# RWKV-7 chunk inverses folded into the chain's stationary operands, one iteration ahead of their use

## The chip, the cores and the metric

The kernel runs on one core of a Trainium2 chip. The metric is device time in microseconds (us), from the start of the program to its end, as the median of several executions. Engines are named as the profile names them: PE is the matrix engine (PEld its weight loads), DVE the vector engine, ACT the scalar engine, POOL the GpSimd engine, SP the engine that only issues transfers. Each runs its instructions in order; they wait for one another by semaphores.

## The reference

One inference step of a one-layer encoder: a gated FFN, one combined input projection, RWKV-7 beside chunk-banded attention, an output projection, a second gated FFN and a last norm. 1024 prompt rows are computed together with 8 streams of 16 rows. The change concerns RWKV-7, a recurrence over tokens for each of 8 heads with a 64x64 state `s`:

```python
def step(s, inp):
    r_t, w_t, k_t, v_t, kk_t, a_t = inp
    sa = jnp.einsum('bhvk,bhk->bhv', s, kk_t)
    s = (s * w_t[:, :, None, :] - sa[..., None] * (kk_t * a_t)[:, :, None, :]
         + v_t[..., None] * k_t[:, :, None, :])
    y_t = jnp.einsum('bhvk,bhk->bhv', s, r_t)
    return s, y_t
```

The kernel does it in chunks of L = 32 tokens. In a chunk the vectors `sa` of the tokens depend on one another through a triangular system, whose inverse (32x32 for each chunk and head) is computed beforehand.

## The kernel before, in words

Everything is written out for one core, as a program whose instructions a scheduler of the framework puts in order for each engine before the kernel runs; the order on an engine is then fixed. The stages are: first FFN, projection and preparation of RWKV, the RWKV chain beside the attention, output projection, second FFN.

**Preparation.** `_project` computes the columns of RWKV and of attention. For each pair of heads p (4) and each group of 8 chunks g (5), `_prepare_products` writes to DRAM what the chain will read: `ard` (rows that multiply the state), `grd` (the masked products of a chunk with itself: of its 64 rows 32 belong to the values, 32 to the solved vectors), `wsd` (the turned keys, also 32 rows for the values and 32 for the solved vectors) and `ad` (the triangular matrices). `_invert` loads up to 112 triangular matrices, one to a partition, inverts them on DVE in 31 steps of two instructions, and stores them as `inv`. Two of the inversions (of p = 3, and of the late groups of p = 2) come after the projection, right ahead of the chain.

**Chain.** `_rwkv` runs 10 iterations of 4 steps, so 40 steps, numbered here 0 to 39 (a step is one chunk of all 8 heads, or 4 of the 16-row streams at the end). `_rwkv_load` brings the operands of one iteration one iteration ahead: `mov` (state in rows 0 to 63, values in rows 64 to 95, solved vectors in rows 96 to 127), `wout` and `wst` (stationary operands with the same rows), and `tt`, the inverses. A step in `_rwkv_run` is: 8 products `pw` (L961) from state and values; a copy to `wx` (L963); 8 products `pu` with the inverses (L966); four copies of `pu` into rows 96 to 127 of `mov`, by DVE and ACT in turn (L969); 8 products `px` (L971) and 8 products `py` (L975); two DVE products that scale `px` into the next state (L984); a copy of `py` to `y` (L986). `pw`, `pu`, `px` lie in one bank called `ps_c`; `py` and all small helpers share one bank, `_post_bank`. `_rwkv_post` normalises the outputs of iteration i - 1 in pieces between the steps of iteration i (POOL subtracts the mean, L1024, and scales, L1032; after the last step PE turns `y`, L1038, DVE multiplies to `yo`, L1042, POOL adds, L1044, SP stores `yo`).

**What stands beside the chain.** Three iterations are written ahead of `_attention_inputs`, whose value projection (`ps_av`, L567 to L569, 432 products) fills PE between the chain's dependent steps. Then memory is freed, and `_attention` runs 74 units on it; six units are written after each further iteration. The loads of attention are issued by POOL (`_attention_load`: `q` L1081, `kt` L1087, `v` L1089, `bias` L1091); they go into memory that `ps_av` reads until its end. Transfers of the projection are issued by SP (`k.dq`) and ACT (`k.aq`); the chain's by SP.

Of the kernel before, what the change touches and what calls it, by code (L numbers as in the profile page):

```python
# [9 lines left out]
F32 = mybir.dt.float32  # L10
# [461 lines left out]
def _project(k, a):  # L472
# [50 lines left out]
    for p in range(NPAIR):  # L523
        srcs = [shifted(4 * j + p) for j in range(3)]
        _prepare_more(k)
        _rwkv_prepare(k, p, wa, *srcs)
        for q in QK[NQK * p // NPAIR:NQK * (p + 1) // NPAIR]:
            _attention_in(k, w, *q)
        if p == 1:
            _invert(k, (0, 0, NG))  # L530
        elif p == 2:
            _invert(k, (1, 0, NG), (2, 0, 2))
    _prepare_more(k)
# [260 lines left out]
def _prepare_products(k, q):  # L794
# [60 lines left out]
def _invert(k, *parts):  # L855


    nc = k.nc
    am = k.iv.tile([P, L, L], F32, tag="inv_a", bufs=k.niv, name="inv_a")
    w = k.iv.tile([P, L, L], F32, tag="inv_w", bufs=k.niv, name="inv_w")  # L860
    n, rows = 0, []
    for p, g0, g1 in parts:
        rows.append(slice(n, n + 16 * (g1 - g0)))
        n += 16 * (g1 - g0)
        nc.sync.dma_start(am[rows[-1]], k.ad[p][g0:g1].rearrange("g h c s t -> (g h c) s t"))
    nc.gpsimd.memset(w, 0.0)
    nc.gpsimd.memset(_flat(w)[:, 0:L * L:L + 1], 1.0)
    for s in range(L - 1):
        r, m = s + 1, L - 1 - s
        u = k.iv.tile([P, r, m], F32, tag="inv_t", bufs=2, name="inv_t")  # L870
        nc.vector.tensor_tensor(u[:n], w[:n, 0:r, s:s + 1].to_broadcast([n, r, m]),
                                am[:n, s:s + 1, s + 1:].to_broadcast([n, r, m]), ALU.mult)
        nc.vector.tensor_tensor(w[:n, 0:r, s + 1:], w[:n, 0:r, s + 1:], u[:n], ALU.add)
    for (p, g0, g1), r in zip(parts, rows):
        nc.sync.dma_start(k.inv[p][:, g0:g1].rearrange("s g x t -> (g x) s t"), w[r])


def _chunk_constants(k, a):
# [7 lines left out]
    for w in k.wst:  # L886
        nc.vector.tensor_copy(w[0:HD].rearrange("r p e i (h d) -> r (p e i h) d", d=HD),
                              k.ident[0:HD, None, 0:HD].to_broadcast([HD, 4 * NH, HD]))


def _rwkv_load(k, i):


# [17 lines left out]
    nc.sync.dma_start(q.wout[0:HD], k.ard[g].rearrange("(h d) c l -> d h c l", d=HD)[:, :, cj])  # L911
    nc.sync.dma_start(q.wout[HD:P].rearrange("r h c l -> r h (c l)"), k.grd[g][:, :, cj].rearrange("h r c l -> r h (c l)"))
    q.wst = k.wst[i % 2]
    for e in range(2):
        nc.sync.dma_start(q.wst[HD:P, :, e].rearrange("r p i x -> r p (i x)"),
                          k.wsd[g][:, HEADS[e], 2 * j:2 * j + 2].rearrange("p r i x -> r p (i x)"))

# [11 lines left out]
def _sample_states(k, a, j, mov):  # L929

    nc = k.nc
    for p in range(NPAIR):
        sin = k.rw.tile([P, 4, HD], F32, tag="sin", bufs=4, name="sin")
# [4 lines left out]
        nc.scalar.copy(mov[0:HD, :, 2 * p:2 * p + 2].rearrange("r b h d -> r b (h d)"),  # L938
                       ps[0:HD].rearrange("p (b x) -> p b x", x=P))


def _rwkv_run(k, a, i, pq, q, nq):
# [4 lines left out]
    q.y = rw.tile([P, 4, 2, HD], F32, tag="y", bufs=2, name="y")  # L947
    post = iter(()) if pq is None else _rwkv_post(k, i - 1, pq)
    fin = None
    if i == 7:  # L950
        fin = rw.tile([HD, 1, NH, HD], F32, tag="y", bufs=2, name="fin")
    for c in range(4):
        cc = 4 * i + c
        mov, wout = q.mov[:, c], q.wout[:, :, c]
        wst = q.wst[:, :, c % 2, c // 2].rearrange("r p (h d) -> r p h d", d=HD)
        pw, pu = (k.cbank[:, 128 * j:128 * j + 128].rearrange("p (a d) -> p a d", a=2)
                  for j in (cc % 2, 1 - cc % 2))
# [12 lines left out]
        for hh in range(NH):  # L970
# [29 lines left out]
def _state_out(k, st, dst):  # L1000
# [13 lines left out]
def _rwkv_post(k, i, q):  # L1014
# [257 lines left out]
def tile_encoder_step(ctx: ExitStack, tc: tile.TileContext, *aps):  # L1272
# [35 lines left out]
    with ExitStack() as s_rw, ExitStack() as s_xg:  # L1308
# [97 lines left out]
        with ExitStack() as s:  # L1406
# [119 lines left out]
```

## Time and profile before

| what | value |
|---|---|
| median of 3 runs | 2608.65 us (2604.74 to 2610.08) |
| time of the profiled execution | 2605.25 us |
| span of the profiled execution | 2603.5 us |
| PE busy in the span | 2422.6 us, 93% |
| DVE, ACT, POOL busy | 1124.8, 899.8, 1076.5 us |
| transfers | 284.75 MB in 230283 packets |

The span is the part of the execution between the first and the last instruction of the core; 1.75 us lie around it. Starts of instructions are counted in us from the start of the span. The granted clock (PEclk) is the mean of two levels of PE's clock, 1.00 for 2.4 GHz and 0.50 for 1.2 GHz. A busy PE isn't a PE at its peak: matmuls overlap, so what a group of matmuls holds of PE is read from its start to the start of the next group.

### The profile page before, as it was taken

The page shows a single profiled execution, that of the slowest core. Times are in us where ns is not written, and L with a number is a line of the kernel's source. Part 1 is how long each engine was busy: PE and PEld are TensorE (multiplying, and loading weights), DVE is VectorE, ACT ScalarE, POOL GpSimd, SP SyncE. Part 2 cuts the span into 40 slices and gives each one's busy share as a digit, 9 for nine tenths or more (in the row PEclk, how much of TensorE's full clock was granted, in tenths as well). Part 3 has the DMA queues.
Part 4 walks back from the last instruction along what each step waited for, and adds up shares of the span by engine and source line. Part 5 has one row for each costly group of instructions (what it writes and reads, how often), then busy time and mean ns, then how long its engine had stood idle before and what let it go on. Part 6 is the DMA issues. An engine that isn't in the chain of part 4 may idle for free.

```text
span 2603.5 us, 43481 instructions
## 1 busy us (share of the span) xinstructions
PE 2422.6 (93%) x17415; PEld 2161.5 (83%) x17415; DVE 1124.8 (43%) x2346; ACT 899.8 (35%) x1903; POOL 1076.5 (41%) x966
## 2 busy tenths in 40 slices
PE   4999999988999999999997999897999999989998
PEld 3899999986888799899874666676999999988886
DVE  6322222214544533856854666346222222225555
ACT  5333333321111443443323576524333333321112
POOL 4545454444433233443213443105554544544332
PEclk8999999999999999999996899998999999999999
DMA  3222112227322324543658994522221122252221
GB/s 113 67 68 86 56 63 86 67 83 269 113 77 70 107 63 133 168 132 104 190 148 197 219 206 112 175 91 65 67 86 57 62 86 68 69 197 102 77 102 73
DMA packets 230283, 284.75 MB, mean 109 GB/s; under 512 B 54920, under 2 KB 183552, under 8 KB 227264
## 3 DMA queue, kind: packets, MB, share of 16 engines
q1 hardware_dynamic: 194044, 226.72, 27.8%
q0 software_dynamic: 7648, 25.43, 4.1%
q10 hardware_dynamic: 28388, 29.81, 3.5%
q8 instruction: 137, 2.24, 0.4%
q14 instruction: 66, 0.54, 0.1%
HBM read 191.79 MB, written 90.12 MB: 108 GB/s over the span
## 4 chain that ended last, share of the span: by engine, by line
PE 42%; DVE 5%; POOL 3%; issue 3%; ACT 2%; DMA 2%; ACTq 0%; POOLq 0%; DVEq 0%
PE pa L341 3%; PE pd L450 3%; PE pd L451 3%; PE pd L449 3%; PE pa L343 3%; PE pa L342 3%; PE pb L341 2%; PE pb L342 2%; PE pb L343 2%; POOL frm L292 2%; PE ps_s L1132 1%; PE ps_o L1186 1%; PE ps_pt L1171 1%; PE ps_yc L975 1%; PE ps_wo L1261 1%
## 5 line engine op out<-in xcount | busy, mean ns | idle before, releaser
L341 PE MATMUL pa<-F,frm 128*128 128x256 f32 (+1 forms) x1408 | 424.6, 302 | 34.7 <-ACT r L348 25.2
L343 PE MATMUL pa<-F,frm 128*128 128x256 f32 (+1 forms) x1408 | 419.3, 298 | 2.7 <-POOL frm L292 2.7
L342 PE MATMUL pa<-F,frm 128*128 128x256 f32 (+1 forms) x1408 | 419.3, 298 | 2.1 <-POOL F L272 2.1
L453 DVE TENSOR_TENSOR x<-pd,x 128x512 f32<-128x512 f32 x396 | 270.0, 690 | 243.1 <-PE pd L451 228.8
L163 POOL TENSOR_TENSOR spl<-raw,spl 128x1024 fp32r<-128x1024 f32 x78 | 187.6, 2408 | 453.0 <-ACT spl L162 453.0
L449 PE MATMUL pd<-spl,h 128*128 128x512 f32 x792 | 314.0, 397 | 14.8 <-ACT spl L162 12.1
L450 PE MATMUL pd<-spl,h 128*128 128x512 f32 x792 | 311.9, 394 | 13.3 <-POOL spl L163 13.3
L292 POOL TENSOR_TENSOR frm<-cmb,frm 128x512 fp32r<-128x512 f32 x176 | 230.1, 1309 | 221.7 <-ACT frm L291 221.3
L343 PE MATMUL pb<-F,frm 128*128 128x320 f32 (+1 forms) x1056 | 312.7, 296 | 3.1 <-POOL frm L292 3.1
L342 PE MATMUL pb<-F,frm 128*128 128x320 f32 (+1 forms) x1056 | 312.2, 296 | 3.1 <-DVE F L271 3.1
L341 PE MATMUL pb<-F,frm 128*128 128x320 f32 (+1 forms) x1056 | 313.3, 297 | 1.2 <-ACT frm L291 1.2
L451 PE MATMUL pd<-spl,h 128*128 128x512 f32 x792 | 311.8, 394 | 0.0
L341 PEld LDWEIGHTS pa<-F,frm 128*128 128x128 f32 x1408 | 268.9, 191 | 44.4 <-ACT r L348 33.0
L343 PEld LDWEIGHTS pa<-F,frm 128*128 128x128 f32 x1408 | 269.1, 191 | 3.5 <-POOL frm L292 3.5
L342 PEld LDWEIGHTS pa<-F,frm 128*128 128x128 f32 x1408 | 269.4, 191 | 2.5 <-POOL F L272 2.5
L292 POOL TENSOR_TENSOR frm<-raw,frm 128x512 fp32r<-128x512 f32 x132 | 173.8, 1318 | 186.7 <-ACT frm L291 186.7
L162 ACT ACTIVATE spl<-raw 128x1024 fp32r<-128x1024 f32 x78 | 82.2, 1055 | 406.3 <-PE pd L451 342.7
L343 PEld LDWEIGHTS pb<-F,frm 128*128 128x128 f32 x1056 | 200.2, 190 | 3.8 <-POOL frm L292 3.8
L342 PEld LDWEIGHTS pb<-F,frm 128*128 128x128 f32 x1056 | 200.1, 190 | 3.3 <-DVE F L271 3.3
L341 PEld LDWEIGHTS pb<-F,frm 128*128 128x128 f32 x1056 | 200.0, 189 | 1.8 <-ACT frm L291 1.8
L449 PEld LDWEIGHTS pd<-spl,h 128*128 128x128 f32 x792 | 150.1, 190 | 48.5 <-ACT spl L162 12.3
L450 PEld LDWEIGHTS pd<-spl,h 128*128 128x128 f32 x792 | 150.1, 189 | 48.3 <-POOL spl L163 16.2
(259 smaller groups left out, 4572.7 us busy)
## 6 DMA issues: line engine op xcount, KB each, us to landing
raw<-in_w_ff_gate_dram SPq DMA_DIRECT2D x22, 1024.0 KB
raw<-in_w_ff_up_dram SPq DMA_DIRECT2D x22, 1024.0 KB
raw<-in_w_ff_down_dram SPq DMA_DIRECT2D x44, 512.0 KB
raw<-in_w_in_dram SPq DMA_DIRECT2D x26, 512.0 KB
hr<-hd SPq DMA_DIRECT2D x11, 1152.0 KB
hr<-he SPq DMA_DIRECT2D x11, 1152.0 KB
q<-qk POOLq DMA_DIRECT2D x24, 384.0 KB, 7.6
x<-xd SPq DMA_DIRECT2D x18, 512.0 KB
```

What stands on the lines that cost most here:

```text
L162: k.nc.scalar.activation(dst[:, 0], raw, AF.Copy)
L163: k.nc.gpsimd.tensor_tensor(dst[:, 1], raw, dst[:, 0].bitcast(F32), ALU.subtract)
L292: nc.gpsimd.tensor_tensor(d[:, 1], x, d[:, 0].bitcast(F32), ALU.subtract)
L341: nc.tensor.matmul(ps, frm[:, 0, c], F[:, 0, jj, c], start=new and c == 0, stop=False, **kw)
L342: nc.tensor.matmul(ps, frm[:, 0, c], F[:, 1, jj, c], start=False, stop=False, **kw)
L343: nc.tensor.matmul(ps, frm[:, 1, c], F[:, 0, jj, c], start=False, stop=c == 3, **kw)
L449: mm(ps, h[:, 0, f, a], d[f][:, 0, b], start=f == 0, stop=False)
L450: mm(ps, h[:, 0, f, a], d[f][:, 1, b], start=False, stop=False)
L451: mm(ps, h[:, 1, f, a], d[f][:, 0, b], start=False, stop=f == 1)
L453: nc.vector.tensor_tensor(xs, ps, xs, ALU.add)
L975: mm(py[s, hh % 2], wout[:, hh, L:], mov[:, hh], start=True, stop=True)
L1132: mm(ps, q.qs[i // 3][:, j, h, t:t + P], q.ks[h][:, c0:c0 + n], start=j == 0, stop=j == 1)
```

## The change

Products with the inverse are no longer made inside a step. Since a solved vector is the inverse times a column of `pw`, and is used only through `wst` and the right half of `wout`, the inverse can be multiplied into those operands instead: `_fold` does it for iteration i + 1 during steps 0 and 1 of iteration i, in two halves of 32 products each (`kg`, keys, 64 columns; `gq`, 32 columns), a copy of each half (`fk` by ACT, `fq` by DVE) and four transfers of each on SP that move the rows to partitions 96 to 127. `_fold_load` brings `tt`, `kg` and `gq`. A step then is `pw`, four copies on DVE alone, `px`, `py`, state. The preparation writes `gqd` (2 transfers on SP for each p and g) and `kgd` (2 on ACT), and `wsd` goes from SP to ACT; `_rwkv_load` brings half as many rows of `grd` and `wsd`. The inversion works on the transposed result, with the same element counts. Of the last inversion only loads and memsets come ahead of the chain; its DVE work is written after the chain's first iteration, and one more iteration is written ahead of the attention's inputs (4 instead of 3). Eight units are written after each iteration instead of six. Some small tiles share a buffer: `gn_sq` now lies in the buffer of `yo`, `so` in that of `sin`.

```diff
@@ _prepare_products
     for h in range(2):
+        k.dq.dma_start(k.gqd[g][L * p:L * p + L, h], gram[HD * h + L:HD * h + 2 * L, :, L:])
...
-    k.dq.dma_start(k.wsd[g][p], tb)
+    nc.scalar.dma_start(k.wsd[g][p], tb)
+    for e in range(2):
+        nc.scalar.dma_start(k.kgd[g][e, L * p:L * p + L], tb[HD * e + L:HD * e + 2 * L])
@@ _rwkv_load
-    nc.sync.dma_start(q.wout[HD:P].rearrange("r h c l -> r h (c l)"), k.grd[g][:, :, cj].rearrange("h r c l -> r h (c l)"))
+    nc.sync.dma_start(q.wout[HD:HD + L].rearrange("r h c l -> r h (c l)"), k.grd[g][:, :L, cj].rearrange("h r c l -> r h (c l)"))
@@ new
+def _fold(k, i, q):
+    nc = k.nc
+    g, j = divmod(i, 2)
+    tt, kg, gq = k.tt[g], k.kg.pop(i), k.gq.pop(i)
+    ps = _post_bank(k, "ps_f").rearrange("p (e i h d) -> p e i h d", e=2, i=2, h=2)
+    for c in range(4):
+        for h in range(2):
+            for b in range(NPAIR):
+                s = slice(L * b, L * b + L)
+                nc.tensor.matmul(ps[s, c % 2, c // 2, h], tt[s, h, 4 * j + c], kg[s, c % 2, c // 2, HEADS[h]], start=True, stop=True)
+    fk = k.rw.tile([P, 4 * P], F32, tag="fk", bufs=1, name="fk")
+    nc.scalar.copy(fk, ps.rearrange("p e i h d -> p (e i h d)"))
+    for b in range(NPAIR):
+        nc.sync.dma_start(q.wst[HD + L:P, b].rearrange("r e i x -> r (e i x)"), fk[L * b:L * b + L])
+    yield
...
@@ _rwkv_run
-        wx = rw.tile([P, 2, HD], F32, tag="wx", bufs=2, name="wx")
-        nc.vector.tensor_copy(wx, pw)
-        for hh in HEAD_ORDER:
-            s = slice(L * (hh // 2), L * (hh // 2) + L)
-            mm(pu[s, hh % 2], q.tt[s, hh % 2, c], wx[s, hh % 2], start=True, stop=True)
-        for j in range(4):
-            copy = nc.scalar.copy if j % 2 else nc.vector.tensor_copy
-            copy(mov[HD + L:P, 2 * j:2 * j + 2], pu[L * j:L * j + L])
+        for b in range(NPAIR):
+            nc.vector.tensor_copy(mov[HD + L:P, 2 * b:2 * b + 2], pw[L * b:L * b + L])
...
+        if c < 2 and nq is not None:
+            next(fold, None)
+        if c == 2 and i + 2 < 2 * NG:
+            _fold_load(k, i + 2)
@@ _rwkv_post
-    sq = rw.tile([P, NH, HD], F32, tag="gn_sq", bufs=1, name="gn_sq")
+    sq = rw.tile([P, NH, HD], F32, tag="yo", bufs=1, name="gn_sq")
@@ tile_encoder_step
+        next(chain)
+        next(chain)
+        for _ in late:
+            pass
         for _ in range(3):
             next(chain)
...
-                for _ in range(6):
+                for _ in range(8):
                     next(units, None)
```

The first place is PE inside the value projection. Of before, this is what stands from the `pu` of step 3 to two of the pieces of its `py`:

```order
L966 MATMUL ps_c<-wx,tt 32x64 x8
L567 MATMUL ps_av<-spl,xg 128x256
L568 MATMUL ps_av<-spl,xg 128x256
L569 MATMUL ps_av<-spl,xg 128x256
L567 MATMUL ps_av<-spl,xg 128x256
L975 MATMUL ps_yc<-mov,wout 32x64
L568 MATMUL ps_av<-spl,xg 128x256
L569 MATMUL ps_av<-spl,xg 128x256
L975 MATMUL ps_yc<-mov,wout 32x64
```

In the changed program there is no `pu`; here are both fold halves (`ps_f`) for iteration 1, beside step 2 of iteration 0 (L1010 is `pw`, L1014 `px`, L1018 `py`, L569 to L571 the value projection):

```order
L972 MATMUL ps_f<-kg,tt 32x64 x32
L1010 MATMUL ps_c<-mov,wout 32x64 x8
L569 MATMUL ps_av<-spl,xg 128x256
L570 MATMUL ps_av<-spl,xg 128x256
L571 MATMUL ps_av<-spl,xg 128x256
L1018 MATMUL ps_yc<-mov,wout 32x64 x8
L569 MATMUL ps_av<-spl,xg 128x256
L570 MATMUL ps_av<-spl,xg 128x256
L571 MATMUL ps_av<-spl,xg 128x256
L569 MATMUL ps_av<-spl,xg 128x256
L983 MATMUL ps_f<-gq,tt 32x32 x32
L1014 MATMUL ps_c<-mov,wst_12326 64x64 x8
```

Eight products of each step have gone, 64 of each iteration have come, and they stand in runs of 32.

The second place is POOL where the attention begins, after the projection's last work. Before:

```order
L1032 TENSOR_TENSOR y<-y,gn_s 128x512
L1081 DMA q<-qk_8741 64x4x384 x2
L1087 DMA kt<-qk_8844 64x384 x2
L1044 TENSOR_TENSOR yo<-yo,gb 128x512
L1024 TENSOR_TENSOR y<-y,gn_m 128x512
L1087 DMA kt<-qk_8844 64x384 x2
L1089 DMA v<-vd 128x3x128
L1031 TENSOR_TENSOR gn_s<-gn_s,mhalf 128x8
L1091 DMA bias<-bias_6312 128x1024
```

In the changed program the same loads (L1133 `q`, L1139 `kt`, L1141 `v`, L1143 `bias`) read so:

```order
L1091 TENSOR_TENSOR yo<-yo,gb 128x512
L1071 TENSOR_TENSOR y<-y,gn_m 128x512
L1133 DMA q<-qk_8763 64x4x384 x2
L1139 DMA kt<-qk_8866 64x384 x4
L1141 DMA v<-vd 128x3x128
L1143 DMA bias<-bias_6322 128x1024
L1133 DMA q<-qk_8763 64x4x384
L1078 TENSOR_TENSOR gn_s<-gn_s,mhalf 128x8
```

The `yo` that stood between the first loads and the others (that of iteration 1, which needs the end of iteration 2) now stands behind them.

The third place is PE where the value projection has ended. Before, the order from step 9 on is:

```order
L961 MATMUL ps_c<-mov,wout 32x64 x8
L966 MATMUL ps_c<-wx,tt 32x64 x8
L975 MATMUL ps_yc<-mov,wout 32x64 x3
L971 MATMUL ps_c<-mov,wst_12331 64x64 x8
L975 MATMUL ps_yc<-mov,wout 32x64 x5
L961 MATMUL ps_c<-mov,wout 32x64 x8
L966 MATMUL ps_c<-wx,tt 32x64 x8
L975 MATMUL ps_yc<-mov,wout 32x64 x3
```

In the changed program it is, after the `pw` and `px` of step 9 (L1184 are scores, `ps_s`, of the first units, L1223 turns the first unit's weights):

```order
L1184 MATMUL ps_s<-kt,q 128x128 x2
L972 MATMUL ps_f<-kg,tt 32x64 x32
L1010 MATMUL ps_c<-mov,wout 32x64 x8
L1184 MATMUL ps_s<-kt,q 128x128 x2
L1018 MATMUL ps_yc<-mov,wout 32x64 x8
L983 MATMUL ps_f<-gq,tt 32x32 x32
L1014 MATMUL ps_c<-mov,wst_12326 64x64 x8
L1018 MATMUL ps_yc<-mov,wout 32x64 x8
L1184 MATMUL ps_s<-kt,q 128x256 x2
L1010 MATMUL ps_c<-mov,wout 32x64 x8
L1223 MATMUL ps_pt<-ident,e 128x128
```

The scores of the third unit (128x256) stand behind 14 steps' work before (0 to 13), and behind 11 steps' work now (0 to 10).

## Rows read from the trace of the kernel before

**Rows 1.** Windows: stretch, length, busy of PE, PEld, DVE, ACT, POOL, clock, DMA share, GB/s.

```profile
1040.00:1280.00 240.00, 225.49 (x1681) 210.83 (x1680) 165.74 (x429) 98.37 (x225) 100.87 (x136) 0.99 0.47 146
1280.00:1368.00 88.00, 84.67 (x1031) 71.29 (x1035) 56.38 (x158) 16.97 (x51) 11.06 (x8) 0.98 0.63 156
1368.00:1406.00 38.00, 20.42 (x329) 14.17 (x330) 12.89 (x36) 5.32 (x19) 14.63 (x21) 0.57 0.86 192
1406.00:1617.00 211.00, 201.33 (x2638) 139.25 (x2639) 133.39 (x373) 138.35 (x365) 87.09 (x108) 0.87 0.82 185
1617.00:1661.00 44.00, 38.03 (x375) 28.03 (x371) 24.27 (x73) 36.74 (x99) 8.87 (x11) 0.96 0.40 115
```

**Rows 2.** Timeline of step 9: start, length, engine, line, what, [idle before <- releaser].

```profile
1367.92 0.43 PE L961 MATMUL ps_c<-mov,wout 96*32 96x64 f32 x16
...
1368.42 0.29 DVE L963 COPY wx<-ps_c 128x128 f32<-128x128 f32 x1 [0.55 <-PE ps_c L961]
...
1368.77 0.43 PE L966 MATMUL ps_c<-wx,tt 32*32 32x64 f32 x16 [0.41 <-DVE wx L963]
...
1369.26 0.28 DVE L969 COPY mov<-ps_c 32x128 f32<-32x128 f32 x1 [0.55 <-PE ps_c L966]
...
1369.69 0.26 ACT L969 COPY mov<-ps_c 32x128 f32<-32x128 f32 x1 [1.36 <-DVE mov L969]
...
1369.98 0.29 DVE L969 COPY mov<-ps_c 32x128 f32<-32x128 f32 x1 [0.43 <-ACT mov L969]
...
1370.31 0.26 ACT L969 COPY mov<-ps_c 32x128 f32<-32x128 f32 x1 [0.36 <-DVE mov L969]
...
1370.62 0.69 PE L971 MATMUL ps_c<-mov,wst 128*64 128x64 f32 x16
...
1371.23 0.41 PE L975 MATMUL ps_yc<-mov,wout 128*32 128x64 f32 x10
...
1372.33 0.43 PE L961 MATMUL ps_c<-mov,wout 96*32 96x64 f32 x16 [0.69 <-DVE mov L984]
```

**Rows 3.** Timeline of POOL, same columns, from the end of the value projection.

```profile
1368.01 1.49 POOL L1081 DMA_DIRECT2D q<-qk  x2
1369.49 1.07 POOL L1087 DMA_DIRECT2D kt<-qk  x2
1387.86 1.26 POOL L1044 TENSOR_TENSOR yo<-yo,gb 128x512 f32<-128x512 f32 x1 [17.30 <-DVE yo L1042]
...
1391.31 0.79 POOL L1089 DMA_DIRECT2D v<-vd  x1
...
1393.82 0.59 POOL L1091 DMA_DIRECT2D bias<-bias  x1
```

**Rows 4.** Timeline of DVE and PE where the first units begin.

```profile
1404.45 0.50 DVE L1142 TENSOR_TENSOR ps_s<-ps_s,bias 128x128 f32<-128x128 f32 x2 [3.94 <-DMA bias<-bias]
...
1405.81 0.80 PE L1132 MATMUL ps_s<-kt,q 128*128 128x256 f32 x2 [3.21 <-ACT e L1157]
```

**Rows 5.** Timeline of ACT's queue and PE in step 10.

```profile
1377.66 0.32 ACTq L583 DMA_DIRECT2D out_dram<-vt  x1
1378.03 0.26 ACT L969 COPY mov<-ps_c 32x128 f32<-32x128 f32 x1 [3.64 <-DMA out_dram<-vt]
...
1378.34 1.12 PE L971 MATMUL ps_c<-mov,wst 128*64 128x64 f32 x16 [3.15 <-ACT mov L969]
```

**Rows 6.** Timeline of PE inside the value projection.

```profile
1348.75 0.30 PE L975 MATMUL ps_yc<-mov,wout 128*32 128x64 f32 x2
...
1348.98 0.39 PE L568 MATMUL ps_av<-spl,xg 128*128 128x256 f32 x1
...
1361.48 0.43 PE L966 MATMUL ps_c<-wx,tt 32*32 32x64 f32 x16
...
1361.84 0.38 PE L569 MATMUL ps_av<-spl,xg 128*128 128x256 f32 x1
```

**Rows 7.** Timeline of PE: matmuls of 16 columns.

```profile
1480.25 0.99 PE L1194 MATMUL ps_o<-ptr,cv 128*64 128x16 f32 x26
```

**Rows 8.** Transfers from 1280 to 1660: queue, packets, MB, share of 16 engines.

```profile
q1 hardware_dynamic: 51477, 35.09, 40.0%
```

More of the change, by code (lines that the diff above doesn't have):

```diff
@@ L529, in _project @@
         if p == 1:
-            _invert(k, (0, 0, NG))
+            for _ in _invert(k, (0, 0, NG)):
+                pass
         elif p == 2:
-            _invert(k, (1, 0, NG), (2, 0, 2))
+            for _ in _invert(k, (1, 0, NG), (2, 0, 2)):
+                pass
     _prepare_more(k)
@@ L867, in _invert @@
     nc.gpsimd.memset(_flat(w)[:, 0:L * L:L + 1], 1.0)
+    yield
     for s in range(L - 1):
         r, m = s + 1, L - 1 - s
[L870 to L873, printed above, removed]
+        u = k.iv.tile([P, m, r], F32, tag="inv_t", bufs=2, name="inv_t")
+        nc.vector.tensor_tensor(u[:n], w[:n, s:s + 1, 0:r].to_broadcast([n, m, r]),
+                                am[:n, s, s + 1:, None].to_broadcast([n, m, r]), ALU.mult)
+        nc.vector.tensor_tensor(w[:n, s + 1:, 0:r], w[:n, s + 1:, 0:r], u[:n], ALU.add)
     for (p, g0, g1), r in zip(parts, rows):
@@ L911, in _rwkv_load @@
     nc.sync.dma_start(q.wout[0:HD], k.ard[g].rearrange("(h d) c l -> d h c l", d=HD)[:, :, cj])
-    nc.sync.dma_start(q.wout[HD:P].rearrange("r h c l -> r h (c l)"), k.grd[g][:, :, cj].rearrange("h r c l -> r h (c l)"))
+    nc.sync.dma_start(q.wout[HD:HD + L].rearrange("r h c l -> r h (c l)"), k.grd[g][:, :L, cj].rearrange("h r c l -> r h (c l)"))
     q.wst = k.wst[i % 2]
     for e in range(2):
-        nc.sync.dma_start(q.wst[HD:P, :, e].rearrange("r p i x -> r p (i x)"),
-                          k.wsd[g][:, HEADS[e], 2 * j:2 * j + 2].rearrange("p r i x -> r p (i x)"))
+        nc.sync.dma_start(q.wst[HD:HD + L, :, e].rearrange("r p i x -> r p (i x)"),
+                          k.wsd[g][:, HD * e:HD * e + L, 2 * j:2 * j + 2].rearrange("p r i x -> r p (i x)"))
     n = 4 * (L if g < 4 else NQ)
@@ L939, in _sample_states, with _fold_load @@
                        ps[0:HD].rearrange("p (b x) -> p b x", x=P))
+def _fold_load(k, i):
+    nc = k.nc
+    g, j = divmod(i, 2)
+    if j == 0:
+        k.tt[g] = k.rw.tile([P, 2, 8, L], F32, tag="tt", bufs=2, name="tt")
+        nc.sync.dma_start(k.tt[g].rearrange("s a c t -> s (a c t)"), k.inv[:, :, g].rearrange("b s x t -> (b s) (x t)"))
+    k.kg[i] = k.rw.tile([P, 2, 2, P], F32, tag="kg", bufs=1, name="kg")
+    nc.sync.dma_start(k.kg[i].rearrange("s e i x -> s e (i x)"),
+                      k.kgd[g][:, :, 2 * j:2 * j + 2].rearrange("e s i x -> s e (i x)"))
+    k.gq[i] = k.rw.tile([P, 2, 4, L], F32, tag="gq", bufs=1, name="gq")
+    nc.sync.dma_start(k.gq[i].rearrange("s h c l -> s h (c l)"), k.gqd[g][:, :, 4 * j:4 * j + 4].rearrange("s h c l -> s h (c l)"))
+def _fold(k, i, q):
+    nc = k.nc
+    g, j = divmod(i, 2)
+    tt, kg, gq = k.tt[g], k.kg.pop(i), k.gq.pop(i)
[9 more added lines that the diff above has]
+        nc.sync.dma_start(q.wst[HD + L:P, b].rearrange("r e i x -> r (e i x)"), fk[L * b:L * b + L])
+    yield
+    ps = _post_bank(k, "ps_f")[:, :8 * L].rearrange("p (h c l) -> p h c l", h=2, c=4)
+    for c in range(4):
+        for h in range(2):
+            for b in range(NPAIR):
+                s = slice(L * b, L * b + L)
+                nc.tensor.matmul(ps[s, h, c], tt[s, h, 4 * j + c], gq[s, h, c], start=True, stop=True)
+    fq = k.rw.tile([P, 2, 4, L], F32, tag="fq", bufs=1, name="fq")
+    nc.vector.tensor_copy(fq.rearrange("p h c l -> p (h c l)"), ps.rearrange("p h c l -> p (h c l)"))
+    for b in range(NPAIR):
+        nc.sync.dma_start(q.wout[HD + L:P, 2 * b:2 * b + 2, :, L:].rearrange("r h c l -> r (h c) l"),
+                          fq[L * b:L * b + L].rearrange("r h c l -> r (h c) l"))
 def _rwkv_run(k, a, i, pq, q, nq):
@@ L948, in _rwkv_run @@
     post = iter(()) if pq is None else _rwkv_post(k, i - 1, pq)
+    fold = _fold(k, i + 1, nq) if nq is not None else None
     fin = None
@@ L955, in _rwkv_run @@
         wst = q.wst[:, :, c % 2, c // 2].rearrange("r p (h d) -> r p h d", d=HD)
-        pw, pu = (k.cbank[:, 128 * j:128 * j + 128].rearrange("p (a d) -> p a d", a=2)
-                  for j in (cc % 2, 1 - cc % 2))
+        pw = k.cbank[:, 128 * (cc % 2):128 * (cc % 2) + 128].rearrange("p (a d) -> p a d", a=2)
         px = k.cbank[:, 256:].rearrange("p (a d) -> p a d", a=NPAIR)
@@ L961, in _rwkv_run @@
             mm(pw[s, hh % 2], wout[0:HD + L, hh, 0:L], mov[0:HD + L, hh], start=True, stop=True)
-        wx = rw.tile([P, 2, HD], F32, tag="wx", bufs=2, name="wx")
-        nc.vector.tensor_copy(wx, pw)
-        for hh in HEAD_ORDER:
-            s = slice(L * (hh // 2), L * (hh // 2) + L)
-            mm(pu[s, hh % 2], q.tt[s, hh % 2, c], wx[s, hh % 2], start=True, stop=True)
-        for j in range(4):
-            copy = nc.scalar.copy if j % 2 else nc.vector.tensor_copy
-            copy(mov[HD + L:P, 2 * j:2 * j + 2], pu[L * j:L * j + L])
+        for b in range(NPAIR):
+            nc.vector.tensor_copy(mov[HD + L:P, 2 * b:2 * b + 2], pw[L * b:L * b + L])
         for hh in range(NH):
@@ L1054, in _rwkv @@
     n = 2 * NG
+    _fold_load(k, 0)
     pq, q = None, _rwkv_load(k, 0)
     k.nc.vector.memset(q.mov[0:HD, 0], 0.0)
+    for _ in _fold(k, 0, q):
+        pass
+    _fold_load(k, 1)
+    yield
     for i in range(n):
@@ L1298, in tile_encoder_step @@
     k.wsd = [tc.dram_tile([NPAIR, P, 4, P], F32, name=f"wsd{g}") for g in range(NG)]
+    k.kgd = [tc.dram_tile([2, P, 4, P], F32, name=f"kgd{g}") for g in range(NG)]
+    k.gqd = [tc.dram_tile([P, 2, 8, L], F32, name=f"gqd{g}") for g in range(NG)]
     k.vmd = [tc.dram_tile([P, 2, NH * HD], F32, name=f"vmd{g}") for g in range(NG)]
@@ L1390, in tile_encoder_step @@
         s_pr.close()
-        _invert(k, (3, 0, 2))
-        _invert(k, (2, 2, NG), (3, 2, NG))
+        for _ in _invert(k, (3, 0, 2)):
+            pass
+        late = _invert(k, (2, 2, NG), (3, 2, NG))
+        next(late)
         k.rw = pool(s_rw, "rw")
@@ L1395, in tile_encoder_step @@
         chain = _rwkv(k, a)
+        next(chain)
+        next(chain)
+        for _ in late:
+            pass
         for _ in range(3):
```

9 lines of the change are left out of this document (3 added, 6 removed).

## The prediction

> **What bounds the kernel now.** I read the busy time by stage first. In the value projection (1280 to 1368) PE is busy 84.67 of 88 us at a clock of 0.98, though the chain runs through it: the chain's latency is covered there, and only what its instructions hold of PE counts. From 1368 to 1406 PE is busy 20.42 of 38 us, at a clock of 0.57: the cover has ended, attention hasn't begun. From 1406 to 1617 chain and attention share PE (201.33 of 211 us, clock 0.87, the transfers' engines busy 0.82), from 1617 to 1661 units stand alone [rows 1]. So a shorter chain step is worth little for itself, except in the gap of 38 us.
>
> Then I asked for the timeline of the gap. Step 9 starts at 1367.92 and step 10 at 1372.33, 4.41 us: products, copy, products, four copies that take turns on DVE and ACT, products, state [rows 2]. The gap isn't five such steps only. POOL issues `q` and two of four `kt` at 1368.01 and 1369.49, then waits 17.30 us for the `yo` of iteration 1, which has to wait for iteration 2's end, and so `v` goes out at 1391.31 and `bias` at 1393.82 [rows 3]. `bias` lands when DVE can add it, 1404.45, 10.63 us after its issue, and at 1405.81 PE takes the third unit's scores [rows 3, 4]. I call that the restart. Steps 9 to 13 are done by then (five steps), 26 remain. The chain is late too for the last cache stores that ACT issues: step 10's copy sat behind them 3.64 us [rows 5].
>
> **The change part by part.**
>
> *Removed products.* A `pu` holds PE 0.36 us (1361.48 to 1361.84) [rows 6]; 40 of them, 14.4 us.
>
> *Added folds.* A half is 32 products, 64 records, four times the 16 of a `pu` of the same shape: 4 x 0.36 = 1.44 us. For the 32 columns of the second half no row exists. Its price lies between half of that (0.72 us) and the same; 26 records of 16 columns took 0.99 us, 38 ns each, no less than the 27 ns of a record of 64 columns (0.43 us for 16) [rows 6, 7], so I take 1.44. Twenty halves hold 28.8 us: PE gets 14.4 us more work in all. Where it counts depends on the stretch.
>
> *Value projection.* The old order had 9 steps (0 to 8) in it, the new one 8 and six halves. Less 9 x 0.36 = 3.2 us and one step without `pu` (0.36 + 0.61 + 0.41 = 1.4 us: `pw` as `pu`, `px` from 1370.62 to 1371.23, ten records of `py` [rows 2]); more 6 x 1.44 = 8.6 us. Pieces of `py` that stand alone hold 0.23 us for two records (1348.75 to 1348.98 [rows 6]); the order has 54 runs of chain work between `ps_av` before and 39 now. Fifteen fewer at some 0.2 us: -3. Sum +1 us.
>
> *The gap.* In the new order POOL's loads stand ahead of that `yo`; they need the memory of `ps_av`, so they still begin at its end, which I call T0. `q` 1.49 and two `kt` 1.07 us bring the issue to T0 + 2.6 [rows 3]. With the 10.63 us of `bias` as landing time the first scores start near T0 + 12.7; four `kt`, `v` and `bias` are out by T0 + 5.0, so `bias` is there by T0 + 16. PE goes in order, so behind those first scores come two halves, step 10 and the scores between them. Steps 8 and 9 are over by then: without copy and `pu`, a step is 0.50 (to the first copy) + 3 x 0.30 + 0.31 (last copy to `px`) + 1.71 (`px` to next `pw`) = 3.4 us [rows 2]. At the lower clock `px` took 1.12 instead of 0.69 us, 1.6 times as long [rows 2, 5]. So two halves 4.6, `px` 1.1, `pw` and `py` 1.2, scores 1.3: 8.2 us, and the restart at T0 + 21. Before it came 37.9 us after the end of the cover. -17 us. From both sides: if loads land at once, the chain sets it at three steps and two halves, 13 us, -25; if `bias` and the chain's own loads (both use the same engines) land twice as late, T0 + 33, -5.
>
> *After the restart.* Before, 26 steps of 0.36 + 0.36 + 0.61 + 0.41 = 1.74 us: 45.2. Now three steps fewer have been done: 29 of 1.38 = 40.0, and twelve halves 17.3: 57.3. +12 us, if PE is the bound all through; PE idles 9.7 of 211 us there [rows 1], so the least is about +6 (halves that fill idle time, second halves at half price), the most +18 (all of it at the lower clock, 1.6 times 12 being 19).
>
> *Dependence of the chain.* Two hops fewer in each step: at most the 9.7 us of idle time are to be had. I take -2. At the restart PE runs on from the first scores nearly without pause, so the lower clock should end earlier than before; -1.
>
> *Transfers.* Gone for each iteration are 512 packets of 1 KB (half of `grd` and `wsd`); `kg` and `gq` add 512, `fk` 128 of 2 KB, `fq` 1024 of 128 bytes: +1152. The chain's queue used 40% of 16 engines over 380 us for 51477 packets, 47 ns each [rows 8]: 3.4 us of all engines for each iteration, some 20 us beyond the restart, where they are busy 0.82 of 211 us [rows 1]. There is room for it. I cost it at 0, with 0 to +12 as bounds: the cover is that prefetched loads have their time, and it is gone if folded rows land after `px` wants them.
>
> The Trainium skill, "DMA: Bandwidth & Descriptors", puts line rate at 512 bytes or more (Specifications), which speaks against the 128-byte pieces, but says in "Why small descriptors are slow (HBM only)" that transfers within SBUF are spared, a 1 MB one with 128-byte packets reaching 78% of the link. By that and its 435 GB/s, the 384 KB of `fk` and `fq` would take an estimated 1.2 us, and the sum would be the same, for the price above is already 0.
>
> *Preparation.* ACT gets three issues for each of 20 units at about 0.32 us [rows 5], 19 us, over 240 us in which it is busy 98 us and PE 225 [rows 1]; SP gets two and gives one. ACT's evacuations cover it; 0, at most +5. The late inversion has PE covered by `ps_av` as before: 0. `gn_sq` in the buffer of `yo` makes ACT wait for the store of `yo`, with exponentials queued behind it; in the order some 25 DVE instructions lie between that `yo` and the `gn_sq`, so 0; without them up to a landing time, 10 us in each of seven iterations.
>
> **Sum:** +1 - 17 + 12 - 2 - 1 = -7 us on 2605.25, the profiled execution's time: 2598. The median of the runs is 3.4 us above that execution; I keep 2598.
>
> **The rivals.**
>
> *A. The gap shrinks, and nothing is gained.* The loads of attention meet those of the chain when transfers are already at 0.86 of the engines' time [rows 1]; if landing takes as long again, the gap gives 5 to 10 us and the folds take it back: +1 - 8 + 12 - 3 = +2, about 2605 (2600 to 2610). For it: 10.63 us for one 512 KB load. Against: half of the gap before was POOL's own wait.
>
> *B. Slower, by the clock.* PE's clock was at its lower level for 2 x (1 - 0.87) = 26% of the stretch 1406 to 1617 [rows 1], after moments in which PE waited. Runs of 32 products with 32 rows and columns, in one bank that others need, add such moments: each fold waits for the bank's last copy, and `py` for the fold's. If the mean clock falls to 0.79, another 0.16 x 211 = 34 us run at the lower level and lose some 0.4 of it, 13 us: -7 + 13 = +6, 2611; at 0.75, 2618. It decides from about 0.83 down, where the gain is used up. For it: the folds' work is of that kind, and the clock already moves. Against: PE has less to wait for in each step.
>
> The Trainium skill, "TensorE: Matmul & The Clock Gate", section "A second HAM failure mode: psum-queue depth-cycling", says that PE that idles shortly between groups for its banks has its clock swing between the two levels; by that rule B is what comes. The clock of 0.87 at 95% busy agrees with it in kind.
>
> *C. More gain.* Chain and loads land early, folds fill idle time, and the clock returns sooner: -25 + 6 - 4 = -23, 2582.
>
> **How the numbers follow.** The forecast (its own range 2590 to 2603) gets 0.48, A 0.25, B 0.18, C 0.09. About 0.2%, 5.2 us, is what a measurement of this kernel can tell from no change. Faster than 2603.4: 0.42 of the forecast, a little of A, and C, 0.52. Within: 0.27; slower: 0.21. The range leaves out the ends of B and C: 2581 to 2615.
>
> **What would show it.** Right: `ps_f` halves of about 1.4 us at the full clock, 0.43 us `pu` gone; step to step 3.4 us in the gap; `bias` issued within 6 us of the last `ps_av`; the third unit's scores some 21 us after it; PE's work beyond the restart up by about 12 us. Wrong: `ps_s` waiting for `kt` or PE for folded rows far beyond that; a clock under 0.83 from the restart to the chain's end; ACT's `gn_sq` waiting for the store of `yo`; PE idle in the projection well above 14.5 of 240 us.

## The result, and the profile after

The changed kernel takes 2641.43 us (median of 4 runs, 2638.28 to 2653.09) beside 2606.69 us for the kernel before (4 runs): a ratio of 1.0143, 95% interval 1.0106 to 1.018, so about 37 us slower. The forecast was 2598 us and its range ended at 2615. The profiled execution took 2644.2 us, its span 2642.2.

The windows of the changed kernel, with the columns of [rows 1], show where:

```profile
1040.00:1280.00 240.00, 225.00 (x1706) 212.71 (x1706) 163.84 (x428) 97.62 (x225) 98.82 (x136) 0.99 0.55 157
1280.00:1368.00 88.00, 80.96 (x1176) 70.93 (x1173) 54.72 (x154) 12.74 (x32) 6.13 (x4) 0.90 0.61 147
1368.00:1406.00 38.00, 18.54 (x345) 14.55 (x341) 12.62 (x40) 3.92 (x13) 14.56 (x20) 0.60 0.78 174
1406.00:1617.00 211.00, 179.65 (x2499) 130.06 (x2498) 122.25 (x353) 110.00 (x280) 77.65 (x99) 0.79 0.80 183
```

The projection is as before. From 1406 to 1617 PE is busy 179.65 us where it was 201.33, at a clock of 0.79 where it was 0.87 [rows 1]: PE waits, while DMA is no busier (0.80 against 0.82). The last outputs of attention come at 1700.61 instead of 1659.07. PE alone shows this in the gap (timeline, columns of [rows 2]):

```profile
1371.07 0.43 PE L1010 MATMUL ps_c<-mov,wout 96*32 96x64 f32 x16
1383.68 1.22 PE L1014 MATMUL ps_c<-mov,wst 128*64 128x64 f32 x16 [12.17 <-issue]
...
1394.35 1.93 PE L972 MATMUL ps_f<-kg,tt 32*32 32x64 f32 x64 [3.15 <-DMA kg<-kgd]
...
1403.16 0.80 PE L1184 MATMUL ps_s<-kt,q 128*128 128x256 f32 x2
```

The `px` of step 8 stands 12.17 us behind its `pw`; the trace names no releaser for it. It is the first `px` of iteration 2, so it reads the rows that the fold wrote. What SP did at that time (timeline of SP's queue):

```profile
1368.20 0.78 SPq L920 DMA_DIRECT2D wst<-wsd  x2
1374.57 0.55 SPq L926 DMA_DIRECT2D gb<-gb  x1
1375.21 5.26 SPq L976 DMA_DIRECT2D wst<-fk  x4
1380.52 5.98 SPq L987 DMA_DIRECT2D wout<-fq  x4
1386.60 0.55 SPq L955 DMA_DIRECT2D kg<-kgd  x1
```

ACT had copied `fk` at 1354.16, some 20 us earlier, and its four transfers still went out from 1375.21 to 1380.47, when `px` already wanted them. The waits of SP's queue from 1360 to 1392 (total us, times, longest us) name what held it here: the landings of the last cache stores of the value projection, which ACT issues.

```profile
SPq L920 <- DMA out_dram<-vt: 14.8, 1, 14.8
SPq L926 <- DMA out_dram<-vt: 5.5, 1, 5.5
SPq L976 <- DMA out_dram<-vt: 2.8, 2, 1.5
SPq L987 <- DMA out_dram<-vt: 2.3, 1, 2.3
```

In front of `fk` (L976) stands `gb` (L926) too, but the `yo` that it waits for was done at 1372.14, 2.4 us before `gb` went out. In later iterations it is that `yo` that holds the queue (the same view from 1300 to 1700):

```profile
SPq L926 <- POOL yo L1091: 96.7, 7, 20.7
```

`gb` of iteration i + 1 goes into the buffer that `yo` of iteration i - 1 reads (two buffers), and that `yo` is the last work of iteration i. So every fold of iteration i + 1 is sent only when iteration i has ended. The chain of waits around 1450 shows the whole loop (start, length, what):

```profile
1445.08 0.42 PE ps_y L1085 x3
...
1445.76 0.90 DVE yo L1089 x4
...
1446.73 1.27 POOL yo L1091
...
1448.02 0.55 SPq L926
...
1448.61 0.67 SPq L976
...
1451.02 11.37 DMA wout<-fq
...
1462.43 0.42 PE ps_yc L1018 x2
```

From the last transposes of one iteration to the first `py` that may run in the next lie 17.35 us (1445.08 to 1462.43). Before, `gb` (L921 there) waited for the same `yo`, but only loads with an iteration of time stood behind it:

```profile
SPq L921 <- POOL yo L1044: 46.9, 7, 29.2
```

### The profile page after: what moved, and what is told of

It is laid out like the page before. It is cut to its first block, busy times and chain, and to the rows that moved or that the text cites. A ratio compares the mean times of both kernels' runs of the same rounds, so it can differ in the third digit from the quotient of the medians.

```text
span 2642.2 us, 44951 instructions
## 1 busy us (share of the span) xinstructions
PE 2428.2 (92%) x18055; PEld 2177.3 (82%) x18055; DVE 1133.3 (43%) x2396; ACT 881.7 (33%) x1833; POOL 1074.1 (41%) x966
## 4 chain that ended last, share of the span: by engine, by line
PE 68%; DMA 8%; POOL 6%; DVE 6%; issue 6%; ACT 3%; SPq 1%; ACTq 0%; POOLq 0%; DVEq 0%
PE pa L341 6%; PE pd L449 6%; PE pa L343 6%; PE pa L342 6%; PE pd L451 6%; PE pd L450 6%; PE pb L341 3%; PE pb L342 3%; PE pb L343 3%; POOL frm L292 3%; PE ps_p L226 2%; PE ps_p L228 2%; PE ps_p L227 2%; DVE cmb L297 1%; PE ps_wo L1314 1%
```

## The experiments

All ratios are to the kernel before on the same chip; 0.1% is 2.6 us. copy_chain3, copy_u6 and copy_sq stand on `fold_copy`; copy_sq_gb on copy_sq; copy_late0, copy_moves0 and copy_twice on copy_sq_gb; copy_spread on copy_moves0.

| kernel | median us | ratio, 95% interval |
|---|---|---|
| gb_late | 2627.26 | 1.0073 (1.0044 to 1.0102) |
| sq_own | 2643.71 | 1.0133 (1.0102 to 1.0163) |
| gb_sq | 2626.66 | 1.0075 (1.0052 to 1.0097) |
| fold_actq | 2620.39 | 1.0049 (1.0028 to 1.007) |
| gb_actq | 2614.26 | 1.0026 (1.0003 to 1.0049) |
| gb_sq_actq | 2609.64 | 1.0008 (0.9993 to 1.0023) |
| fold_copy | 2611.59 | 1.0024 (0.9999 to 1.0048) |
| copy_chain3 | 2612.51 | 1.0033 (1.0015 to 1.005) |
| copy_u6 | 2611.33 | 1.0014 (0.9988 to 1.0039) |
| copy_sq | 2605.7 | 0.9985 (0.9972 to 0.9999) |
| copy_sq_gb | 2601.47 | 0.9972 (0.9953 to 0.999) |
| copy_late0 | 2602.71 | 0.998 (0.9967 to 0.9994) |
| copy_moves0 | 2596.27 | 0.9959 (0.9945 to 0.9973) |
| copy_spread | 2605.14 | 0.999 (0.9974 to 1.0006) |
| copy_twice | 2667.4 | 1.0234 (1.0216 to 1.0253) |
| after_moves0 | 2641.68 | 1.013 (1.0101 to 1.0158) |
| before_sq | 2618.95 | 1.0024 (1.0005 to 1.0044) |
| before_late | 2618.74 | 1.003 (1.0016 to 1.0044) |

**gb_late, sq_own, gb_sq: which wait.** Theory Q says SP's queue, theory G the shared buffer of `gn_sq`, theory P the folds' products.

```diff
 # gb_late: out of _rwkv_load, into _rwkv_run behind the fold of the same step
+        if c == 1:
+            _gb_load(k, i, q)
 # sq_own (gb_sq has both)
-    sq = rw.tile([P, NH, HD], F32, tag="yo", bufs=1, name="gn_sq")
+    sq = rw.tile([P, NH, HD], F32, tag="gn_sq", bufs=1, name="gn_sq")
-    fk = k.rw.tile([P, 4 * P], F32, tag="fk", bufs=1, name="fk")
+    fk = k.rw.tile([P, 4 * P], F32, tag="kg", bufs=1, name="fk")
```

gb_late: 

> The changed kernel with one transfer moved: gb of an iteration is loaded in its own iteration, behind the transfers of its fold, and not one iteration ahead in front of them. Theory Q (SP's queue): the load of gb waits for the yo of two iterations before (96.7 us in 7 waits, after), and fk and fq stand behind it, so folded rows go out when px already wants them. Then px of step 8 waits under 4 us (12.17 before the edit), the chain and units end 25 to 35 us earlier, and the time is 2607 to 2617, about that of the kernel before. Theory G (gn_sq in yo's buffer): the chain of waits goes through the store of yo (four of 8 to 10 us); little changes, 2632 to 2641. Theory P (the products of the folds and the clock): within 5 us of 2641.

sq_own: 

> The changed kernel with gn_sq in a buffer of its own again; to make room fk lies in the buffer of kg, so the next kg waits for the landing of fk. Theory Q: gn_sq is late only because SP is late; 2636 to 2644. Theory G: ACT no longer waits for the store of yo, four pieces of 8 to 10 us leave the chain of waits, 2605 to 2620. Theory P: within 5 us of 2641.

gb_sq: 

> Both edits together: gb behind the folds, and gn_sq in its own buffer with fk in that of kg. Theory Q: as with gb moved alone, within 4 us. Theory G: as with gn_sq apart, or if both count, a further 8 to 20 us below the better of the two. Theory P: still 2636 or more. If neither wait remains and the terms of the forecast hold otherwise, 2595 to 2605.

Moving one load takes back about half of the loss (1.0143 to 1.0073: 18 us, 6 to 30 by the two intervals). Q holds, but not in size: 10 us above its range, and the `px` of step 8, which was to wait under 4 us, still waits 8.60 and 2.10 in gb_late (timeline of PE):

```profile
1379.65 1.67 PE L1018 MATMUL ps_c<-mov,wst 128*64 128x64 f32 x12 [8.60 <-issue]
1383.41 0.48 PE L1018 MATMUL ps_c<-mov,wst 128*64 128x64 f32 x4 [2.10 <-DMA wst<-fk]
```

So the wait of step 8 is hardly `gb`'s, and the gain comes later in the chain; that is argued from these rows, not tried apart. A buffer for `gn_sq` takes back nothing, alone or with it, so G isn't borne out here; `fk` in the buffer of `kg` may cost something of its own, which wasn't tried apart. With `gb` out of the way SP waits for the `fk` copy itself (68.0 us in 7 in gb_sq), and all its other transfers queue behind that.

**fold_actq, gb_actq, gb_sq_actq: another queue.**

```diff
-        nc.sync.dma_start(q.wst[HD + L:P, b].rearrange("r e i x -> r (e i x)"), fk[L * b:L * b + L])
+        nc.scalar.dma_start(q.wst[HD + L:P, b].rearrange("r e i x -> r (e i x)"), fk[L * b:L * b + L])
 # and so for the four of fq
```

fold_actq: 

> The changed kernel with the eight transfers of fk and fq of each iteration issued by ACT and not by SP; gb stays where it is. Theory Q: they no longer stand behind gb, but ACT issues 8 transfers per iteration at 0.33 us, 2.6 us, in front of its exponentials, and waits for DVE's fq; 2612 to 2628, so most of what moving gb gives. Theory G: 2641 or more, since ACT still waits for the store of yo. Theory P: within 5 us of 2641.

gb_actq: 

> The changed kernel with both edits of the first runs: gb behind the folds, and fk and fq issued by ACT. Theory L: gb is already out of the way when ACT issues, so nothing is gained over ACT's queue alone; what is left is the landing; 2616 to 2624. If gb in front of the other loads of SP's queue still costs: 2608 to 2615. Theory P: 2618 or more, too.

gb_sq_actq: 

> The changed kernel with transfers kept, and with all three cures: gb behind the folds, gn_sq in a buffer of its own (fk in that of kg), fk and fq issued by ACT. If only the queue made the rows late: as copy_sq_gb, 2598 to 2606. If landing (10.44 and 13.38 us for fq, in gb_actq) and ACT's time for eight issues count as well: 2608 to 2618.

Off SP's queue alone 1.0049, with `gb` moved 1.0026 (the intervals overlap), with `gn_sq` apart as well 1.0008. From gb_sq (1.0075) to gb_sq_actq, which differ by the queue alone, lie 17 us. Even so it lies in the range in which landing and ACT's issues count as well, above that in which only the queue does.

**fold_copy: no transfer at all.** Copies can move rows between partitions, as those into `mov` do.

```diff
-    nc.scalar.copy(fk, ps.rearrange("p e i h d -> p (e i h d)"))
     for b in range(NPAIR):
-        nc.sync.dma_start(q.wst[HD + L:P, b].rearrange("r e i x -> r (e i x)"), fk[L * b:L * b + L])
+        copy = nc.scalar.copy if b % 2 else nc.vector.tensor_copy
+        copy(q.wst[HD + L:P, b].rearrange("r e i x -> r (e i x)"),
+             ps[L * b:L * b + L].rearrange("p e i h d -> p (e i h d)"))
 # the same for the second half, into q.wout
```

> The changed kernel in which the folded rows are moved from the bank to partitions 96 to 127 by four copies of each half (DVE and ACT in turn) and not by a copy and four transfers: 8 copies instead of 2 in each iteration, some 3 us more on DVE and ACT together, no fk and no fq transfer. gb stays in front. Theory L (the folded rows are late because they travel as transfers: issue on a busy queue, then landing): px and py no longer wait for rows; the terms of the forecast hold otherwise, 2595 to 2608, and no wait of PE in the chain over 3 us remains between 1370 and 1400. Theory P (what is left after moving gb or the queue, 2620 to 2627, is the work of the folds on PE and the clock): 2618 or more.

2611.59: above the range of theory L, below that of P; the wait of step 8 is gone, though. What stood in its place is in the timelines of ACT and of PE in this kernel:

```profile
1484.25 0.63 ACT L1072 ACTIVATE gn_sq<-y 128x512 f32<-128x512 f32 x1 [10.97 <-DMA mix<-yo]
1484.78 0.25 ACT L1249 COPY am<-ps_o 128x128 f32<-128x128 f32 x1
```

```profile
1485.09 0.48 PE L1222 MATMUL ps_pt<-ident,e 128*128 128x128 f32 x1 [10.53 <-ACT am L1249]
```

ACT waits 10.97 us for the store of `yo`, a copy of attention stands behind it, and PE stands still 10.53 us for that copy.

**copy_sq, copy_sq_gb, before_sq: the shared buffer again.** Their edits are those of sq_own (without that on `fk`, which is gone) and gb_late; before_sq makes the change's edit on `gn_sq` in the kernel before.

copy_sq: 

> The kernel of fold_copy with gn_sq in a buffer of its own (the memory of fk and fq is free there). In fold_copy ACT waited 10.97 us for the store of yo before a gn_sq at 1484.25, and the chain of waits goes through that store for 19.17 us. Theory G2 (the shared buffer costs once the rows are no longer late): 6 to 14 us below fold_copy (2611.59), 2597 to 2606, so as fast as the kernel before or faster. Theory P (what is left is the folds' work on PE): within 4 us of fold_copy.

copy_sq_gb: 

> The same with gb loaded behind the folds too, so that no transfer of SP's queue stands behind its wait. If prefetch behind gb is late as well (wst from wsd, kg): a further 3 to 8 us, 2592 to 2601. If gb only hurt the folded rows: within 4 us of copy_sq.

before_sq: 

> The kernel before, with one part of the change alone: gn_sq in the buffer of yo. Theory G2: ACT waits for the store of yo with exponentials queued behind it, 5 to 12 us slower than before. If SP's queue has to be late first (theory Q): within 3 us of before.

copy_sq gains 10 us on fold_copy (1.0024 to 0.9985), within G2's range, and before_sq loses 6 (1.0024; its interval, 1 to 11 us, leaves the size open). So the shared buffer costs about as much as one wait in kernels that wait for no late rows; where rows are late, no gain from curing it was seen. That `gb` gives 3 us more in copy_sq_gb isn't shown; the intervals overlap.

**The moves: copy_chain3, copy_u6, copy_late0, copy_moves0, before_late, after_moves0.** The late inversion, the fourth iteration ahead and the eight units, undone or done alone.

```diff
 # copy_moves0, after_moves0 (chain3, u6 and late0 are its parts)
+        for _ in late:
+            pass
         next(chain)
         next(chain)
-        for _ in late:
-            pass
-        for _ in range(3):
+        for _ in range(2):
...
-                for _ in range(8):
+                for _ in range(6):
```

copy_chain3: 

> The kernel of fold_copy with one iteration fewer written ahead of the attention's inputs (3 as in the kernel before, and not 4). The forecast's term for the gap (the loads of attention go out before the yo of an iteration stops POOL) comes from this edit: without it the gap is long again, 8 to 17 us slower than fold_copy. If the gap gives nothing here: within 4 us of fold_copy.

copy_u6: 

> The kernel of fold_copy with six units of attention written after each iteration, as before, and not eight. The chain then ends later than the units' loop has work for: if the count of units matters for cover, 5 to 15 us to either side of fold_copy; the forecast gave it no term, so by it within 4 us.

copy_late0: 

> The kernel of copy_sq_gb with the last inversion's DVE work ahead of the chain again. If the late inversion is what cost the kernel before 8 us: 4 to 8 us faster than copy_sq_gb, 2593 to 2598. By the forecast (its place costs nothing): within 4 us of 2601.

copy_moves0: 

> The kernel of copy_sq_gb with all three moves undone: inversion ahead of the chain, three iterations ahead of the attention's inputs, six units after each iteration. If the moves cost as in the kernel before: 2591 to 2597, and the folds alone are worth 12 to 17 us. If the folds need the moves for their gain (the forecast's gap): 2604 to 2612.

before_late: 

> The kernel before, with only the parts that move: late inversion behind the chain's first iteration, four iterations ahead of the attention's inputs and not three, eight units after each iteration. No folds. The forecast gave the inversion's place 0 and took the shorter gap from what the folds let the chain do; in this order a yo still stands between the attention's loads on POOL. Forecast's terms: within 5 us of before. If the moved parts are what costs the rest (the chain late beside more units): 5 to 15 us slower.

after_moves0: 

> The changed kernel with nothing but the three moves undone: the last inversion ahead of the chain, three iterations ahead of the attention's inputs, six units after each iteration. If the moves cost by themselves, as in the kernel before (8 us) and in copy_sq_gb (5 us): 2633 to 2637. If the late rows set the time whatever the order around them: within 4 us of 2641.

On the kernel before the moves cost 8 us (4 to 11). Elsewhere no difference is larger than its interval: 2 and 3 us for the parts, 3 us for all three in copy_moves0, 3 us in after_moves0. Where rows are late, the order around them makes no difference that could be seen (after_moves0 leaves some 12 us either way open). copy_moves0, which is the folds with copies and little else, beats both kernels: 0.9959, 11 us below the kernel before (7 to 14).

**copy_twice, copy_spread: what the products cost.**

```diff
 # copy_twice, in both halves, on copy_sq_gb
+                for _ in range(2):
+                    nc.tensor.matmul(ps[s, h, c], tt[s, h, 4 * j + c], gq[s, h, c], start=True, stop=True)
 # copy_spread, on copy_moves0: first half here, the second in the same way
+    for i2 in range(2):
+        ps = _post_bank(k, "ps_f")[:, :256].rearrange("p (e h d) -> p e h d", e=2, h=2)
+        for c in (2 * i2, 2 * i2 + 1):
...
+        yield
...
-        if c < 2 and nq is not None:
+        if nq is not None:
```

copy_twice: 

> The kernel of copy_sq_gb with each product of the folds made twice into the same place: 64 more products in each iteration, 640 in all; at the 1.10 and 0.75 us of a half in the trace of after (1.93 and 1.08 at the lower clock) 19 to 30 us more on PE. If PE is the bound after the restart (forecast +12 for twelve halves, five more lie in the value projection): 10 to 20 us slower than copy_sq_gb, 2611 to 2621. If the folds lie in time in which PE waits: within 6 us.

copy_spread: 

> The kernel of copy_moves0 with each fold in four pieces of 16 products, one behind each step, instead of two runs of 32; the same products, twice as many copies of half the size. If a run of 32 small products uses up PE's instructions faster than they come (the pauses in which PE waits for nothing shown, 8 to 9 us in copy_moves0): they shrink to some 3 us, and 3 to 7 us are gained, 2589 to 2593. If the pauses come with the number of instructions and not with the runs: within 4 us of 2596. Against: 40 more copies, and the last rows come only at the end of the iteration; if that counts, slower by 3 to 10 us.

copy_twice is 68 us above copy_sq_gb; the expectations held at most 20. PE in that kernel (timeline), and its waits of kind "issue" (waiting for nothing that the profile shows) from 1280 to 1740, in part:

```profile
1410.41 1.59 PE L989 MATMUL ps_f<-gq,tt 32*32 32x32 f32 x98 [0.39 <-ACT y L1034]
1416.60 0.68 PE L989 MATMUL ps_f<-gq,tt 32*32 32x32 f32 x30 [4.60 <-issue]
...
1449.39 0.32 PE L1015 MATMUL ps_c<-mov,wout 96*32 96x64 f32 x1
1454.08 0.65 PE L1015 MATMUL ps_c<-mov,wout 96*32 96x64 f32 x13 [4.37 <-issue]
```

```profile
PE ps_f L989 <- issue: 17.3, 6, 4.9
PE ps_c L1015 <- issue: 12.1, 3, 4.6
```

In the middle of independent products PE stops for 4.60 us. All such waits sum to 41.7 us here and 10.6 us in copy_sq_gb; the kernel before has none. (The label alone doesn't tell what PE waits for: the 12.17 us of step 8, a wait for rows, bear it too. The last section says what goes with these.) So of 68 us up to 31 are these pauses, 19 to 30 the products themselves, and the rest is open. copy_spread, which also gives `gq` a second buffer, was to shorten the runs: its pauses sum to 6.5 us against 9.5 in copy_moves0, but it is 8 us slower, as much as it allowed for the added copies and the later rows, with one wait of 11.0 us of a fold piece for ACT's copy of `py` out of the bank they share. That shorter runs save time isn't borne out.

## Why the prediction was wrong

**The step that failed** is *Transfers*: "I cost it at 0, with 0 to +12 as bounds: the cover is that prefetched loads have their time, and it is gone if folded rows land after `px` wants them." I priced packets (3.4 us of all engines per iteration) and never put `fk` and `fq` into SP's order, where they stand behind `gb`, whose wait was in the trace before (46.9 us), and behind the landings of other transfers. They aren't prefetched loads: they are made one iteration ahead, but sent when that iteration has ended, or, for step 8, when the cache stores have landed. The condition was named and left unpriced: 17.35 us in the loop shown, and 1.0143 to 1.0073 for moving `gb` alone. By fold_copy, which has no transfer, the rows' travel cost 1.0143 - 1.0024, some 31 of 37 us (19 to 43 by the two intervals). The Trainium skill, "DMA: Bandwidth & Descriptors", "Why small descriptors are slow (HBM only)", spares transfers within SBUF; by it I had an estimated 1.2 us for both. Here the first `fq` transfer alone, 32 KB, took 11.37 us from issue to landing, with the engines busy 0.80 of the stretch, so a time worked out from that share of the link doesn't price this place.

**gn_sq, 0.** I named it with the right size, 10 us, and set it to 0 because DVE work lies between. That work doesn't cover the store. In fold_copy POOL ends that `yo` at 1464.11, the store goes out 0.9 us later and lands at 1484.16 (chain of waits), and ACT waits 10.97 us of it:

```profile
1464.99 19.17 DMA mix<-yo
```

In the changed kernel itself curing it gave nothing; that the late rows hid it is likely, not shown.

**The gap, -17.** The third unit's scores start at 1403.16; the value projection ends at 1371.15 (1370.87 and 0.28 us of its last matmul). That is 32.0 us, not 21; before 37.9. The gain is 6 us, near the end of my bounds (-5), and it is bought with less chain: 11 steps have their `px` by then, before 14. POOL issued `bias` at 1386.34, T0 + 15 and not + 5, after a wait of 8.91 us before the second pair of `kt`. In copy_sq_gb POOL's loads stand behind a `yo` again, `bias` goes out at 1393.49, and the restart is at 1406.22. It comes no earlier than before (1405.81), but 16 steps are done by then. copy_chain3 takes back the order that this term rests on; it was to cost 8 to 17 us and costs 2, within the intervals.

**After the restart, +12, and the halves.** A half took 1.10 and 0.75 us at the full clock (1.93 and 1.08 at the lower), not 1.44 each: 18.5 us for twenty, not 28.8. The pauses that go with them, 10.6 us in copy_sq_gb, weren't in my sum. How much of both lies in time in which PE would wait isn't settled.

**The value projection, +1.** It ends 3 us later; PE is busy 80.96 of 88 us there. Of the 7.0 us of idle time 3.51, in front of a `px` at 1360.61, are a pause of the kind told of in the last section, and 2.4 a wait of `pw` for the state. **Preparation, 0:** PE idles 15.0 of 240 us, before 14.5. Right.

**Rival A.** Its sum, +2, makes 2607 and not the 2605 that stands there; nothing rests on it. **Rival B.** The clock fell to 0.79, below my 0.83. copy_sq_gb makes the same products without the waits; its window from 1406 to 1617, with the columns of [rows 1]:

```profile
1406.00:1617.00 211.00, 181.00 (x2784) 132.52 (x2784) 144.10 (x417) 133.80 (x342) 95.58 (x118) 0.88 0.81 183
```

The clock is 0.88, so the folds of this kernel don't by themselves bring the lower clock: B had the sign, but its cause isn't borne out, and what does bring it isn't shown. It isn't idle time as such: PE idles 30.0 of 211 us here and 31.4 in the changed kernel. And copy_twice, with twice the products and no late rows, shows 0.78 in the same window, with PE busy 161.37 us.

**The sum.** copy_sq_gb comes out 7 us below the kernel before (3 to 12), which was my sum, and that is luck: it takes copies, a moved load and a buffer that my sum did not have, the restart comes no earlier, and what got shorter is the chain. Its last `py` starts at 1588.5 instead of 1614.6 (tile `ps_yc`; of the kernel before and of copy_sq_gb, first and last start):

```profile
L975 PE MATMUL ps_yc<-mov,wout x640: 216/243/317, 1307.6 to 1614.6; 128*32 128x64 f32 x160
```

```profile
L1021 PE MATMUL ps_yc<-mov,wout x640: 216/219/317, 1324.8 to 1588.5; 128*32 128x64 f32 x160
```

In the changed kernel it starts at 1675.9. The last outputs of attention gain only 1.5 us of that in copy_sq_gb (1657.61 against 1659.07) and 10 us in copy_moves0 (1649.24).

## What to carry to other kernels

Work that is made ahead is ahead only if it is also sent ahead: write down, for each new transfer, what stands before it on its queue and what that waits for, above all a load that waits for a buffer. A buffer shared to make room joins two queues; ask who stands behind the one that waits. A short move between partitions may be cheaper as copies than as transfers behind other loads: 8 copies in place of 2 copies and 8 transfers were worth some 31 us here.

## What the runs showed of the hardware

PE can stop for 2 to 5 us in the middle of independent small products. In the pause from 1449.7 to 1454.08 of copy_twice one packet of the queue for instructions lies, in the window from 1450.5 to 1451.5 (transfers: queue, packets, MB, share):

```profile
q8 instruction: 1, 0.02, 8.1%
```

The trace has the start and length of each packet. This one, of 16 KB, lies from 1451.28 to 1452.58, and PE goes on 1.5 us after its end. The pause from 1412.0 to 1416.60 holds one from 1414.02 to 1415.28, and PE goes on 1.3 us after it. Such packets are common (43 in this kernel from 1340 to 1740), so one in a pause would say little; but in copy_twice every one of the 13 pauses over 1.5 us with the label "issue", 40.7 us in all, ends 1.3 to 1.7 us after the end of such a packet. So do the two in each of copy_sq_gb, copy_moves0 and copy_spread (1.3 to 1.6 us), and in the changed kernel three of four (3.51, 3.63 and 3.21 us); the fourth, the 12.17 us of step 8, has no such packet in it. The kernel before has no such pause. That PE waits there for its own code is what these times say; no run changes the supply of code alone. The Trainium skill, "Runtime: NRT & Kernel Launch", "Instruction fetch mechanics", calls the fetch of each block mostly hidden; this trace disagrees: 40.7 us of such pauses in copy_twice.
